# V terms of the context's expert sum at the delta net's priority on TensorE, and the lower parts of the query weights formed on VectorE

## The chip, the core and the metric

One core of a Trainium2 chip runs the whole program. The metric is the device time of one execution in microseconds. Five engines matter here: TensorE (PE, its weight loads PEld), VectorE (DVE), ScalarE (ACT), GpSimd (POOL) and the DMA queues, of which GpSimd issues the indirect ones and SyncE (SP) nearly all of the others. Each engine works through its own instructions in the order in which they were written into its queue; an instruction that waits holds up all that stand behind it on that engine.

## What is computed

Two layers over 512 latent tokens and 256 context tokens of width 1024. Layer 0 mixes with neighbourhood attention and a gated delta net, layer 1 with latent attention. Each layer ends with the same channel mixer, for latent tokens and (in layer 0) for context tokens, in which a token picks 16 experts per head among 16,384:

```
def peer_ffn(h, w_q, sub_keys, u_tab, v_tab):
    def one_block(xb):                                  # 128 tokens
        qy = (xb @ w_q).reshape(t, PEER_HEADS, 2, PEER_DKEY // 2)
        s = jnp.einsum('thpd,hpnd->thpn', qy, sub_keys)
        s_top, i_top = lax.top_k(s, kk)                 # 16 of 128, per half
        comb = s_top[:, :, 0, :, None] + s_top[:, :, 1, None, :]
        c_top, c_idx = lax.top_k(comb..., kk)           # 16 of 256
        expert = i1 * PEER_KEYS + i2
        gate = jax.nn.softmax(c_top, axis=-1)
        u, vv = u_tab[expert], v_tab[expert]
        act = jax.nn.gelu(jnp.einsum('td,thkd->thk', xb, u))
        return jnp.einsum('thk,thkd->td', gate * act, vv)
```

The delta net's scan, the other piece that the change touches, goes chunk by chunk: `u = w_v - w_k @ s; o = q_dec @ s + p_in @ u; s = b_end * s + k_end.T @ u`, after a triangular solve in each chunk.

## The kernel before

The program is traced in Python and a list scheduler then sorts the instructions of each engine by priority and estimated readiness. Priority falls with the place in the program; `high_priority(offset=k)` moves what is written under it ahead by k places. `LATER` is 4,194,304 (line 30), and `later()` (line 1231) is `high_priority(offset=-LATER)`: whatever stands under it comes last among what could run.

*Routes.* `peer_route` (from line 1030) finds each token's experts: `cp` for the 256 context tokens, `xp` and `yp` for the latent tokens of layers 0 and 1. Its queries are 16 feature blocks in four groups of four. For each block `query` loads a 1024x128 weight (`wq`), rounds it on ScalarE to the upper part (`wqh`, line 1068), subtracts to get the lower part (`wql`, line 1069), and runs 24 matmuls (`qy`). `choose` then scores the group against the sub-keys (`s`, copied to `sc`), and `top16` on VectorE reads each score row several times (`V`, `I`, `t_rep`). The four groups go one after the other: group 0's top-16 runs on VectorE while TensorE makes group 1's queries.

*Two ways to apply experts.* The context's two 128-token tiles, and one latent tile a layer, gather rows: `gather_slots` (from line 1227) yields, tile by tile, 128 steps of U and then 128 of V. Each step has GpSimd gather 128 rows of 1024 floats (512 KB) into one of six `row` buffers (line 1239); four steps later the row is used. A U row is one dot product on VectorE (`cp_jk`, line 1257). A V row is one multiply-add into an accumulator on VectorE (`cp_acc`, line 1282), but while the latent delta net runs (`self.spare`, set in `gdn`), every third one is a pair of matmuls on TensorE instead: ScalarE makes a diagonal matrix of the factors (`cp_dg`, line 1266) and TensorE adds diagonal times row into two banks (`cp_va`, line 1271). 18 V terms of the context's first tile go that way. The gather and the use of a row both stand under `later()`.

The other three latent tiles of each layer run all experts: `peer_dense` goes through 128 blocks, each with 512 KB of U and of V loaded by SyncE, scores, gates, and products on TensorE. ScalarE's rounding of each V block (`vh`, line 1410) marks one block in the trace; VectorE subtracts to get `vl` (line 1411).

*Pace of the gather.* A step is taken from the gather's queue by `pump(anchor, k)`: the gather then may not be issued ahead of the anchor instruction (an order only, no wait at run time), and k says how many steps to take. In the dense layer, each block takes three. `pump(x, 0)` takes none and only sets the anchor; that is what line 1069 does.

*Stages* (us in the trace): context route 335 to 500; latent mixer of layer 0 from there, with the delta net's projections 680 to 823, its scan in four parts (`x_c0` to `x_c3`, starting at 823, 882, 938 and 991) and the output projection (`x_o0` to `x_o3`, from 1074); latent route 1143 to 1503 with the first top-16 at 1179; dense layer 0 from 1519; mixer of layer 1 2560 to 2957; its route 2957 to 3322; dense layer 1 from there to the end.

Of the kernel before, what the change touches and what calls it, by code (L numbers as in the profile page):

```python
# [29 lines left out]
LATER = 1 << 22  # L30
# [10 lines left out]
class Trunk:  # L41
# [988 lines left out]
    def peer_route(self, layer, nm, xT, nd, beside=iter(())):  # L1030


        nc = self.nc
# [4 lines left out]
        with ExitStack() as st:  # L1038
# [10 lines left out]
            def half(t, g):  # L1049
                hs = slice(4 * g, 4 * g + 4)  # L1050
                return self.combine(c1, c2, V[t], Iu[t], ex[t], gate[t], hs, nm + f"_c{t}{g}")

            with ExitStack() as qst:
                w3 = qst.enter_context(self.tc.tile_pool(name=nm + "_prw", bufs=2))
                self.fills(1)
                q2 = qst.enter_context(self.tc.tile_pool(name=nm + "_prq", bufs=2))

                def query(fg):
                    sk = q2.tile([P, 4, P], F32, tag="sk", name=nm + f"_sk{fg}")
                    nc.sync.dma_start(sk, self.I["peer_sk"][layer, :, fg * 4:fg * 4 + 4, :])  # L1060
                    qy = q2.tile([P, 4, n], F32, tag="qy", name=nm + f"_qy{fg}")
                    for j in range(4):
                        f = fg * 4 + j
                        raw, wh, wl = [w3.tile([P, KD, P], dt, tag=tag, name=nm + f"_{tag}{f}")
                                       for tag, dt in (("wq", F32), ("wqh", F32R), ("wql", F32R))]
                        nc.sync.dma_start(raw, self.I[f"peer_w_q{layer}"][:, f * P:(f + 1) * P]
                                          .rearrange("(k p) n -> p k n", p=P))
                        nc.scalar.copy(wh, raw)
                        self.pump(nc.gpsimd.tensor_sub(wl, raw, wh), 0)
                        p = self.ps(nm + f"_qy{fg}{j}")  # L1070
                        for k in range(KD):
                            self.mm(p[:, :n], wh[:, k, :], xh[:, k, :], start=(k == 0), stop=False)
                            self.mm(p[:, :n], wh[:, k, :], xl[:, k, :], start=False, stop=False)
                            self.mm(p[:, :n], wl[:, k, :], xh[:, k, :], start=False, stop=(k == KD - 1))
                        nc.scalar.copy(qy[:, j, :], p[:, :n])
                        aside(1)
                    return qy, sk

                def choose(fg, qy, sk):
                    for t in order:  # L1080
                        p = self.ps(nm + f"_s{fg}_{t}")
                        for j in range(4):
                            self.mm(p[:, j * P:(j + 1) * P], qy[:, j, t * P:(t + 1) * P], sk[:, j, :])
                        sc = q2.tile([P, 4, P], F32, tag="sc", name=nm + f"_sc{fg}_{t}", bufs=4)
                        nc.scalar.copy(sc, p.rearrange("p (j k) -> p j k", k=P))
                        for j in range(4):
                            f = fg * 4 + j
                            self.top16(p2, sc[:, j, :], V[t][:, f, :], Iu[t][:, f, :], P, nm + f"_t{fg}{t}{j}")
                        aside(1)

                first = []

                def aside(k):
                    while k and first:
                        if next(first[0], 0) == 0:
                            first.pop(0)
                        else:
                            k -= 1

                for fg in range(4):  # L1100
                    choose(fg, *query(fg))
                    if fg == 2:
                        next(beside, None)
                    if fg == 1:
                        first += [half(t, 0) for t in order]
                while first:
                    aside(1)
                    self.fills(2)
# [118 lines left out]
    def gather_slots(self, xs, dst, routes, s, layer, nm):  # L1227
        nc, tc = self.nc, self.tc
# [32 lines left out]
        def v_use(act, gate, acc, j, t):  # L1261
            def use(v):
                if self.spare and j % 3 == 0 and 0 < j < P - 8:

                    dg = gp.tile([P, P], F32, tag="diag", name=nm + f"_dg{t}_{j}", bufs=2)
                    nc.scalar.mul(dg, self.ident, act[:, j:j + 1])
                    f, l = self.spare is True, j + 3 >= P - 8
                    if f:
                        self.spare = [self.acc(nm + f"_va{t}{h}") for h in range(2)]
                    for h, p in enumerate(self.spare):  # L1270
                        i = nc.tensor.matmul(p, dg, v[:, h * 512:(h + 1) * 512], start=f, stop=l)  # L1271
                    if l:
                        for h, p in enumerate(self.spare):
                            nc.vector.tensor_add(acc[:, h * 512:(h + 1) * 512], acc[:, h * 512:(h + 1) * 512], p)
                        self.spare = None
                    return i
                if j == 0:
                    nc.scalar.activation(act, act, AF.Gelu)
                    nc.vector.tensor_mul(act, act, gate)
                    i = nc.vector.tensor_scalar_mul(acc, v, act[:, 0:1])  # L1280
                else:
                    i = nc.vector.scalar_tensor_tensor(acc, v, act[:, j:j + 1], acc, op0=ALU.mult, op1=ALU.add)  # L1282
                if j == P - 1:
                    g2 = self.bcast(gp, layer, 2, 1, s, nm + f"_g2{t}", "row", bufs=6)
                    nc.vector.tensor_mul(acc, acc, g2)
                    x = gp.tile([P, D], F32, tag="row", name=nm + f"_gx{t}", bufs=6)
                    nc.sync.dma_start(x, xs[t])
                    nc.vector.tensor_add(acc, x, acc)
                    nc.sync.dma_start(dst[t], acc)
                return i  # L1290
            return use

        for t, (h2, idx, gate) in enumerate(routes):
            act = gp.tile([P, P], F32, tag="act", name=nm + f"_act{t}", bufs=2)
# [384 lines left out]
```

## Time and profile before

| | us |
|---|---|
| median of 3 runs (lowest, highest) | 4307.02 (4299.18, 4308.93) |
| the profiled execution, its own time | 4297.03 |
| its span on the core | 4295.0 |
| PE busy | 3966.5 (92%) |
| DVE busy | 3301.4 (77%) |
| POOL busy | 1725.9 (40%) |
| ACT busy | 1623.1 (38%) |

The mean granted clock of TensorE is 0.968 of full speed. Busy shares are means over stages with different limits, so a change in one stage is read from that stage's own rows. On the page, POOL's costliest work is the gathers (1.25 to 1.44 us of issuing each), and its longest waits are for row buffers to come free: 319.4 us ahead of the context's U gathers, 289.3 us ahead of its V gathers. DMA moved 1113.66 MB in all.

### The profile page before, as it was taken

The page shows a single profiled execution, that of the slowest core. Times are in us where ns is not written, and L with a number is a line of the kernel's source. Part 1 is how long each engine was busy: PE and PEld are TensorE (multiplying, and loading weights), DVE is VectorE, ACT ScalarE, POOL GpSimd, SP SyncE. Part 2 cuts the span into 40 slices and gives each one's busy share as a digit, 9 for nine tenths or more (in the row PEclk, how much of TensorE's full clock was granted, in tenths as well). Part 3 has the DMA queues.
Part 4 walks back from the last instruction along what each step waited for, and adds up shares of the span by engine and source line. Part 5 has one row for each costly group of instructions (what it writes and reads, how often), then busy time and mean ns, then how long its engine had stood idle before and what let it go on. Part 6 is the DMA issues. An engine that isn't in the chain of part 4 may idle for free.

```text
span 4295.0 us, 58812 instructions
## 1 busy us (share of the span) xinstructions
PE 3966.5 (92%) x20522; PEld 3209.9 (75%) x20522; DVE 3301.4 (77%) x7027; ACT 1623.1 (38%) x2947; POOL 1725.9 (40%) x1435
## 2 busy tenths in 40 slices
PE   7997888999899979999999978999999999999998
PEld 4676654687476768888888856775667899999987
DVE  1354988986699979999998886554998777777776
ACT  2353443355124623333333323552245333333333
POOL 0003366543330057777876663001100555555540
PEclk8999998999999989999999988999999999999999
DMA  9835498755634599999999997112246998998885
GB/s 307 293 113 148 161 323 305 284 189 172 204 117 147 220 392 394 396 395 390 394 382 356 331 347 254 47 45 91 78 160 239 362 309 304 309 311 307 308 301 192
DMA packets 484713, 1113.66 MB, mean 259 GB/s; under 512 B 38720, under 2 KB 256320, under 8 KB 475200
## 3 DMA queue, kind: packets, MB, share of 16 engines
q1 hardware_dynamic: 328752, 561.49, 38.0%
q0 software_dynamic: 147600, 537.40, 34.5%
q10 hardware_dynamic: 8064, 11.01, 0.7%
q8 instruction: 162, 2.65, 0.3%
q14 instruction: 135, 1.11, 0.1%
HBM read 1036.30 MB, written 73.92 MB: 258 GB/s over the span
## 4 chain that ended last, share of the span: by engine, by line
PE 56%; DVE 16%; DMA 14%; issue 7%; POOL 5%; ACT 2%; SPq 0%; POOLq 0%; DVEq 0%; ACTq 0%
PE yp_acc L77 11%; PE yp_sp L77 10%; PE xp_sp L77 4%; PE xp_acc L77 3%; DMA cp_u<-peer_u,cp_idx 3%; POOL xp_v L1239 2%; PE mq_s L77 2%; PE x_p L77 2%; DMA xp_u<-peer_u,xp_idx 2%; DMA xp_v<-peer_v,xp_idx 2%; DMA xp_ur<-peer_uT 1%; PE xp_pg L77 1%; PE yp_pg L77 1%; DMA xp_vr<-peer_v 1%; PE c_p L77 1%
## 5 line engine op out<-in xcount | busy, mean ns | idle before, releaser
L1239 POOL DMA_INDIRECT cp_u<-peer_u,cp_idx x256 | 318.9, 1246 | 319.4 <-DVE cp_jk L1257 236.2
L1239 POOL DMA_INDIRECT cp_v<-peer_v,cp_idx x256 | 329.1, 1286 | 289.3 <-PE cp_va L1271 100.3
L77 PE MATMUL xp_sp<-xp_xT,xp_uh 128*128 128x384 f32 x1600 | 409.9, 337 | 16.0 <-ACT xp_ge L1476 14.0
L77 PE MATMUL yp_sp<-yp_xT,yp_uh 128*128 128x384 f32 x1600 | 412.2, 339 | 3.5 <-ACT yp_uh L1372 1.8
L1316 POOL COPY tick<-yp_vh 128x1 f32<-128x1 f32 x104 | 117.5, 1130 | 518.2 <-ACT yp_vh L1410 518.2
L77 PE MATMUL xp_acc<-xp_vh,xp_ah 128*128 128x512 f32 x768 | 305.0, 397 | 20.7 <-ACT xp_ah L1421 20.6
L77 PE MATMUL xp_acc<-xp_vh,xp_al 128*128 128x512 f32 x768 | 307.9, 401 | 15.5 <-DVE xp_al L1422 14.8
L1282 DVE SCALAR_TENSOR_TENSOR cp_acc<-cp_v,cp_act,cp_acc 128x1024 f32<-128x1024 f32 x236 | 302.3, 1281 | 19.4 <-DMA cp_v<-peer_v,cp_idx 17.1
L77 PEld LDWEIGHTS xp_sp<-xp_xT,xp_uh 128*128 128x128 f32 x1600 | 293.0, 189 | 24.6 <-ACT xp_ge L1476 14.6
L77 PE MATMUL xp_acc<-xp_vl,xp_ah 128*128 128x512 f32 x768 | 303.6, 395 | 0.4 <-DVE xp_vl L1411 0.3
L77 PE MATMUL yp_acc<-yp_vh,yp_al 128*128 128x512 f32 x768 | 299.7, 390 | 2.1 <-DVE yp_al L1422 2.0
L77 PEld LDWEIGHTS yp_sp<-yp_xT,yp_uh 128*128 128x128 f32 x1600 | 292.3, 187 | 12.1 <-ACT yp_ge L1476 2.3
L77 PE MATMUL yp_acc<-yp_vh,yp_ah 128*128 128x512 f32 x768 | 299.3, 390 | 0.7 <-ACT yp_ah L1421 0.7
L77 PE MATMUL yp_acc<-yp_vl,yp_ah 128*128 128x512 f32 x768 | 299.1, 389 | 0.0
L1411 DVE TENSOR_TENSOR yp_vl<-yp_vr,yp_vh 128x1024 fp32r<-128x1024 f32 x128 | 156.8, 1225 | 152.8 <-ACT yp_vh L1410 152.7
L77 PE MATMUL yp_sp<-yp_xT,yp_ul 128*128 128x384 f32 x800 | 270.9, 339 | 0.9 <-DVE yp_ul L1373 0.9
L77 PE MATMUL xp_sp<-xp_xT,xp_ul 128*128 128x384 f32 x800 | 270.0, 338 | 0.0
L1421 ACT CAST xp_ah<-xp_a 128x384 fp32r<-128x384 f32 x128 | 65.7, 513 | 431.8 <-DVE xp_a L1417 415.3
L1372 ACT CAST yp_uh<-yp_ur 128x1024 fp32r<-128x1024 f32 x100 | 105.1, 1051 | 294.8 <-PE yp_sp L77 270.6
L1239 POOL DMA_INDIRECT xp_v<-peer_v,xp_idx x128 | 184.8, 1444 | 54.7 <-DVE xp_acc L1282 33.2
L1239 POOL DMA_INDIRECT xp_u<-peer_u,xp_idx x128 | 178.5, 1394 | 64.2 <-DVE xp_jk L1257 30.8
L77 PEld LDWEIGHTS xp_acc<-xp_vh,xp_al 128*128 128x128 f32 x768 | 145.6, 190 | 65.0 <-DVE xp_al L1422 35.0
(1483 smaller groups left out, 10543.9 us busy)
## 6 DMA issues: line engine op xcount, KB each, us to landing
xp_ur<-peer_uT SPq DMA_DIRECT2D x128, 512.0 KB, 6.9
xp_vr<-peer_v SPq DMA_DIRECT2D x128, 512.0 KB, 7.0
yp_ur<-peer_uT SPq DMA_DIRECT2D x128, 512.0 KB, 5.4
yp_vr<-peer_v SPq DMA_DIRECT2D x128, 512.0 KB, 4.4
aw<-ada_w SPq DMA_DIRECT2D x48, 1024.0 KB, 6.9
gdram<-xp_go SPq DMA_DIRECT2D x12, 2048.0 KB, 7.5
xp_gb<-gdram SPq DMA_DIRECT2D x32, 768.0 KB, 11.4
gdram<-yp_go SPq DMA_DIRECT2D x12, 2048.0 KB, 7.1
```

The source lines that it names most:

```text
L77: self.nc.tensor.matmul(out, lhsT, rhs, start=start, stop=stop)
L1239: d = nc.gpsimd.indirect_dma_start(out=r, out_offset=None, in_=tab, in_offset=bass.IndirectOffsetOnAxis(ap=idx[:, j:j + 1], axis=0))
L1282: i = nc.vector.scalar_tensor_tensor(acc, v, act[:, j:j + 1], acc, op0=ALU.mult, op1=ALU.add)
L1316: self.pump(self.nc.gpsimd.tensor_copy(t, src[:, 0:1]), k)
L1372: nc.scalar.copy(uh, uv)
L1411: nc.vector.tensor_sub(vl, vr, vh)
L1421: nc.scalar.copy(ah, a)
```

## The change

Two edits. The diagonal and the two matmuls of a TensorE V term are written under `high_priority(offset=LATER)`, inside the `later()` that already surrounds every use of a row: the two cancel, and these instructions get the priority of the place at which they are written, in the delta net's scan. The gather of the row, and all VectorE uses, stay under `later()`. And `wql` is subtracted on VectorE instead of GpSimd, in all three routes, 16 times each; it remains the anchor.

```diff
@@ -1066,7 +1066,7 @@
                         nc.scalar.copy(wh, raw)
-                        self.pump(nc.gpsimd.tensor_sub(wl, raw, wh), 0)
+                        self.pump(nc.vector.tensor_sub(wl, raw, wh), 0)
@@ -1263,12 +1263,14 @@
                     dg = gp.tile([P, P], F32, tag="diag", name=nm + f"_dg{t}_{j}", bufs=2)
-                    nc.scalar.mul(dg, self.ident, act[:, j:j + 1])
+                    with tc.high_priority(offset=LATER):
+                        nc.scalar.mul(dg, self.ident, act[:, j:j + 1])
                     f, l = self.spare is True, j + 3 >= P - 8
                     if f:
                         self.spare = [self.acc(nm + f"_va{t}{h}") for h in range(2)]
-                    for h, p in enumerate(self.spare):
-                        i = nc.tensor.matmul(p, dg, v[:, h * 512:(h + 1) * 512], start=f, stop=l)
+                    with tc.high_priority(offset=LATER):
+                        for h, p in enumerate(self.spare):
+                            i = nc.tensor.matmul(p, dg, v[:, h * 512:(h + 1) * 512], start=f, stop=l)
```

TensorE before, at the end of the output projection (`x_o3p` products of the last tile, `h2T` transposes of the normed tiles), where the last V term stands:

```order
L77 MATMUL x_o3p_9188<-x_wo_8995,x_yT 128x512 x4
L77 MATMUL x_o3p_9188<-x_wo_8999,x_yT 128x512 x4
L80 MATMUL x_o2h2T_9218<-ident,x_o2h 128x128 x4
L80 MATMUL x_o2h2T_9226<-ident,x_o2h 128x128 x4
L1271 MATMUL cp_va_6511<-cp_v_117_7135,cp_dg_117_7193 128x512
L80 MATMUL x_o3h2T_9234<-ident,x_o3h_9215 128x128 x4
L80 MATMUL x_o3h2T_9241<-ident,x_o3h_9215 128x128 x4
```

TensorE after, in the delta net's third part (`x_c2`, the steps of its triangular solve), where the same term and the one before it stand:

```order
L77 MATMUL x_c2pt_7866<-x_c2X,x_c2Bm 128x128 x4
L1273 MATMUL cp_va_6511<-cp_v_114_7053,cp_dg_114_7140 128x512
L77 MATMUL x_c2py_7872<-x_c2dec,x_c2Y 128x128 x4
L1273 MATMUL cp_va_6510<-cp_v_117_7135,cp_dg_117_7193 128x512
L77 MATMUL x_c2py_7878<-x_c2dec,x_c2Y 128x128 x4
L80 MATMUL x_c2px_7884<-ident,x_c2X 128x128 x4
L77 MATMUL x_c2pt_7908<-x_c2X,x_c2Bm 128x128 x2
L1273 MATMUL cp_va_6511<-cp_v_117_7135,cp_dg_117_7193 128x512
L77 MATMUL x_c2pt_7908<-x_c2X,x_c2Bm 128x128 x2
```

The last V term moved from behind the output projection into the third of the scan's four parts, between matmuls of its chain.

GpSimd before, at the latent route's first `wql` (the context's last V gathers, its second tile's first U gathers):

```order
L1239 DMA cp_v_122_7199<-peer_v,cp_idx_3765 128x1024
L1239 DMA cp_v_123_7202<-peer_v,cp_idx_3765 128x1024
L1069 TENSOR_TENSOR xp_wql_9313<-xp_wq_9311,xp_wqh_9312 128x1024
L1239 DMA cp_v_124_7219<-peer_v,cp_idx_3765 128x1024
L1239 DMA cp_v_125_7222<-peer_v,cp_idx_3765 128x1024
L1069 TENSOR_TENSOR xp_wql_9345<-xp_wq_9343,xp_wqh_9344 128x1024
L1239 DMA cp_v_126_7225<-peer_v,cp_idx_3765 128x1024
L1239 DMA cp_v_127_7228<-peer_v,cp_idx_3765 128x1024
L1239 DMA cp_u_0_7258<-peer_u,cp_idx_3833 128x1024
```

GpSimd after, at the latent route's end (`xp_gk` is the copy of its gates, the last thing before the dense layer):

```order
L1239 DMA cp_u_104_8594<-peer_u,cp_idx_3833 128x1024
L1239 DMA cp_u_105_8598<-peer_u,cp_idx_3833 128x1024
L1118 COPY xp_gk_10744<-xp_gate_9293 128x128
L1239 DMA cp_u_106_8602<-peer_u,cp_idx_3833 128x1024
L1239 DMA cp_u_107_8606<-peer_u,cp_idx_3833 128x1024
```

Of the second tile's 128 U gathers, 106 stand ahead of that copy now, and 22 before the change.

VectorE before, at the first tile of the output projection (`x_o0t` scales the product, `x_o0x` adds the input, `x_o_*` and `x_o0h` norm it):

```order
L1274 TENSOR_TENSOR cp_acc_5507<-cp_acc_5507,cp_va_6510 128x512
L738 TENSOR_TENSOR x_o0t_9021<-x_o0p_9012,x_g_9001 128x512
L739 TENSOR_TENSOR x_o0x<-x_o0x,x_o0t_9021 128x512
L738 TENSOR_TENSOR x_o0t_9033<-x_o0p_9024,x_g_9001 128x512
L739 TENSOR_TENSOR x_o0x<-x_o0x,x_o0t_9033 128x512
L121 TENSOR_SCALAR x_o_v<-x_o_ssq 128x1
L124 RECIPROCAL x_o_y<-x_o_y 128x1
L126 TENSOR_TENSOR x_o_t<-x_o_y 128x1
```

VectorE after, at the second tile of it (`xp_xT` is the transposed normed tile that the route reads):

```order
L739 TENSOR_TENSOR x_o1x<-x_o1x,x_o1t_9065 128x512
L748 TENSOR_TENSOR x_o0h<-x_o0h,x_SH_9007 128x1024
L1257 SCALAR_TENSOR_TENSOR cp_jk_52_7966,cp_act_7257<-cp_u_52_7922,c_o1h_2503 128x1024
L1257 SCALAR_TENSOR_TENSOR cp_jk_53_7970,cp_act_7257<-cp_u_53_7926,c_o1h_2503 128x1024
L738 TENSOR_TENSOR x_o1t_9077<-x_o1p_9068,x_g_9001 128x512
L1257 SCALAR_TENSOR_TENSOR cp_jk_54_7974,cp_act_7257<-cp_u_54_7930,c_o1h_2503 128x1024
L739 TENSOR_TENSOR x_o1x<-x_o1x,x_o1t_9077 128x512
L759 TENSOR_TENSOR xp_xT_8988<-x_o0h2T_9098,xp_xT_8987 128x4x128
```

U rows of the second context tile stand between the projection's own steps, where none stood. In whole stretches: from `x_c1` to `x_o0`, 55 V rows where 42 were and 44 U rows where none were; from `x_o0` to the route's first top-16, 48 U rows where 10 were, none of the 13 V rows that were there, and 6 `xp_wql`; in the route's top-16, 8 U rows where 6 were, and 10 `xp_wql` (4, 4 and 2 ahead of its second, third and fourth group).

VectorE after, in the route of layer 1, between the top-16 of group 0 (`yp_V_24583`) and that of group 1 (`yp_V_24584`):

```order
L1146 MATCH_REPLACE yp_t_rep<-yp_V_24583,yp_sc_2_24840 128x128
L1069 TENSOR_TENSOR yp_wql_24935<-yp_wq_24933,yp_wqh_24934 128x1024
L1147 MAX yp_V_24583<-yp_t_rep 128x8
L1069 TENSOR_TENSOR yp_wql_24967<-yp_wq_24965,yp_wqh_24966 128x1024
L1148 MAX_INDEX yp_I_24587<-yp_V_24583,yp_t_rep 128x8
L1069 TENSOR_TENSOR yp_wql_25126<-yp_wq_25124,yp_wqh_25125 128x1024
L1069 TENSOR_TENSOR yp_wql_25169<-yp_wq_25167,yp_wqh_25168 128x1024
L1143 MAX yp_V_24584<-yp_sc_3_25002 128x8 x2
```

The first two are the lower parts of group 1's third and fourth block: TensorE can finish group 1's queries only when VectorE has come to the end of group 0's top-16.

## Rows read from the trace of the kernel before

**Rows 1.** Page, span in 40 slices: VectorE's busy tenths, the DMA engines' busy tenths.

```profile
DVE  1354988986699979999998886554998777777776
...
DMA  9835498755634599999999997112246998998885
```

**Rows 2.** Windows: stretch, length, PE, PEld, DVE, ACT, POOL busy, PEclk, DMA share, GB/s.

```profile
740.00:830.00 90.00, 85.75 (x345) 56.52 (x343) 85.14 (x115) 32.59 (x57) 65.02 (x67) 0.99 0.92 333
823.00:882.00 59.00, 48.10 (x341) 44.59 (x341) 52.30 (x73) 26.34 (x60) 27.07 (x23) 0.86 0.66 219
882.00:938.00 56.00, 52.72 (x415) 47.14 (x414) 43.19 (x69) 29.01 (x70) 19.67 (x17) 1.00 0.54 174
938.00:991.00 53.00, 52.94 (x418) 47.54 (x417) 39.92 (x67) 29.85 (x71) 18.51 (x15) 1.00 0.42 133
991.00:1074.00 83.00, 77.61 (x503) 60.55 (x502) 59.99 (x112) 40.66 (x116) 33.74 (x28) 0.98 0.61 191
1074.00:1143.00 69.00, 53.42 (x148) 25.72 (x147) 42.28 (x65) 12.34 (x24) 11.87 (x7) 0.89 0.46 145
1143.00:1179.00 36.00, 31.81 (x146) 25.82 (x145) 22.91 (x31) 8.87 (x13) 24.90 (x18) 0.92 0.90 306
1179.00:1268.00 89.00, 78.51 (x364) 64.57 (x363) 88.89 (x508) 23.64 (x35) 37.02 (x20) 0.96 0.40 126
1268.00:1503.00 235.00, 226.99 (x1199) 166.69 (x1199) 234.13 (x795) 118.60 (x238) 7.27 (x5) 0.99 0.48 176
1519.00:1622.00 103.00, 85.12 (x404) 74.21 (x403) 82.68 (x125) 30.33 (x42) 65.02 (x53) 0.92 1.03 387
1622.00:2406.00 784.00, 760.03 (x3762) 675.80 (x3761) 723.19 (x908) 259.78 (x362) 566.13 (x444) 1.00 1.01 383
3403.00:4151.00 748.00, 748.00 (x3777) 685.01 (x3776) 579.88 (x694) 269.14 (x360) 399.26 (x315) 1.00 0.90 308
```

**Rows 3.** Waits, 882 to 1144 and 882 to 1074 us: total, times, longest.

```profile
POOL cp_v L1239 <- PE cp_va L1271: 100.3, 10, 54.7
...
PE cp_va L1271 <- DMA cp_v<-peer_v,cp_idx: 2.6, 1, 2.6
```

**Rows 4.** One line's instructions, 823 to 1503 us: ns least/median/most, first and last start.

```profile
L1257 DVE SCALAR_TENSOR_TENSOR cp_jk<-cp_u,c_o1h x22: 1214/1224/3267, 1158.8 to 1502.2; 128x1024 bf16<-128x1024 f32 x22
...
L1282 DVE SCALAR_TENSOR_TENSOR cp_acc<-cp_v,cp_act,cp_acc x74: 1272/1280/1287, 822.1 to 1148.3; 128x1024 f32<-128x1024 f32 x74
```

**Rows 5.** The same view, rounding of V blocks, one per dense block, in three stretches.

```profile
L1410 ACT CAST xp_vh<-xp_vr x11: 1040/1046/1051, 1519.0 to 1621.5; 128x1024 fp32r<-128x1024 f32 x11
...
L1410 ACT CAST xp_vh<-xp_vr x91: 1032/1049/1055, 1621.5 to 2405.6; 128x1024 fp32r<-128x1024 f32 x91
...
L1410 ACT CAST yp_vh<-yp_vr x90: 1046/1047/1048, 3402.8 to 4143.2; 128x1024 fp32r<-128x1024 f32 x90
```

**Rows 6.** The same view: the subtraction on GpSimd, and its like on VectorE.

```profile
L1069 POOL TENSOR_TENSOR xp_wql<-xp_wq,xp_wqh x16: 2380/2412/2991, 1131.1 to 1249.5; 128x1024 fp32r<-128x1024 f32 x16
...
L1411 DVE TENSOR_TENSOR xp_vl<-xp_vr,xp_vh x128: 1212/1221/1227, 1524.3 to 2544.1; 128x1024 fp32r<-128x1024 f32 x128
```

**Rows 7.** Timeline, 1125 to 1140 us: start, duration, engine, instruction [idle before].

```profile
1131.13 2.99 POOL L1069 TENSOR_TENSOR xp_wql<-xp_wq,xp_wqh 128x1024 fp32r<-128x1024 f32 x1 [4.35 <-DMA x<-x_o3x]
1131.84 2.30 DVE L130 TENSOR_TENSOR x_o_r<-x_o_y,x_o_t 128x1 f32<-128x1 f32 x1
...
1137.65 3.35 DVE L748 TENSOR_TENSOR x_o3h<-x_o3h,x_SH 128x1024 f32<-128x1024 f32 x1
```

**Rows 8.** Timeline, 3008 to 3022 us, and the chain there (start, length, engine).

```profile
3010.12 0.28 DVE L1148 FIND_INDEX8 yp_I<-yp_V,yp_t_rep 128x8 uint32<-128x128 f32 x1
...
3017.44 0.49 DVE L1143 MAX8 yp_V<-yp_sc 128x8 f32<-128x128 f32 x2 [7.04 <-ACT yp_sc L1085]
...
2992.47 22.40 PE yp_qy L77 x96
```

## The prediction

> **What bounds the kernel now.** I read the page's slices first: VectorE is full through the context's gather and again in the latent route, the DMA engines are full in the dense layer of layer 0 and have room while the delta net runs [rows 1]. Then the table by stage, to see which engine each stage waits for. In the projections, 740 to 830, VectorE is busy 85.14 of 90 us (94.6%) with TensorE; at the scan's first part 52.30 of 59 (89%); from 882 to 1074 it falls to 43.19 + 39.92 + 59.99 = 143.10 of 192 us, with DMA at 0.42 to 0.61 [rows 2]. So there is room in the scan, and the waits say who leaves it empty: GpSimd waited 100.3 us ahead of V gathers for the TensorE terms, 54.7 us of it in one piece [rows 3]. In the output projection and up to the first top-16 (1074 to 1179) VectorE does 42.28 + 22.91 = 65.19 of 105 us. In the route's top-16 it is the bound, 88.89 of 89 and 234.13 of 235 us [rows 2].
>
> In dense layer 0 the DMA engines are the bound: a block takes (1621.5 - 1519.0)/10 = 10.3 us over the first ten, then (2405.6 - 1621.5)/90 = 8.71 us, at 383 to 387 GB/s and a share of 1.01 to 1.03. In layer 1 a block takes (4143.2 - 3402.8)/89 = 8.32 us with TensorE busy for 748.00 of 748 us and DMA at 0.90 [rows 2, 5]. What the gathers cost layer 0 against that pace is 10 x 2.0 + 90 x 0.39 = 55 us. That is the most that rows moved out of it can give back.
>
> **V terms at the delta net's priority.** The 36 matmuls and 18 diagonals are the same; what moves is their place, and with it when row buffers come free. GpSimd then runs on: by the orders VectorE gets 13 more V rows and 44 more U rows between x_c1 and x_o0. At 1.280 and 1.224 us [rows 4] that is 16.6 + 53.9 = 70.5 us, and 143.1 + 70.5 = 213.6 us of work for a stretch of 192. VectorE takes its queue in order, so what stands ahead of x_o0 is done ahead of it: the stretch grows by 22 us even if VectorE never idles. At the 94.6% of the projections it takes 225.8 us, **+34**; at the 89% of the scan's first part 240, **+48** [rows 2]. The scan's steps hand over between TensorE and VectorE, so some idling stays; but a row of 1.2 us fits its gaps, as in the projections. I take **+37**, near the first, ends +22 and +48. If TensorE's chain were all that counts, the 70 us would be hidden and the term nought; I don't use that, since 213.6 us of work don't fit into 192.
>
> From x_o0 to the route's first top-16: 38 more U rows (46.5 us), 13 V rows fewer (-16.6), six subtractions come to VectorE at 1.221 us [rows 6] (7.3), and three long stretches there go (next part, -6.3): 65.2 + 46.5 - 16.6 + 7.3 - 6.3 = 96.1 of 105 us, 92%. It fits, but rows now stand between the norms of four tiles that the route waits for. **+3**, ends 0 (all in gaps) and +12 (ten rows in the way).
>
> In the dense layer 28 U rows of the second tile are left at its start instead of 128 - 22 = 106 [rows 4]. Before, the surplus over the three rows a block was worked off slowly over nearly all blocks. After, by VectorE's order it is gone after some 17 blocks, and the rest runs at three rows, as in layer 1. If the first ten blocks stay as slow and seven more lose 0.39, 23 us of the 55 remain: gain 32. If the first ten shrink with the surplus (28/106 of 20 us), 8 remain: gain 47. If only the later loss shrinks, in step with rows, 35 x 78/106 = 26. I take **-38**, ends -26 and -50.
>
> **Lower parts on VectorE.** 48 subtractions of 2.41 us leave GpSimd, 48 of about 1.22 us (the like for `vl`) come to VectorE [rows 6]: 58.6 us in all, priced by where they fall. Something comes back: where a GpSimd subtraction overlapped a VectorE instruction with two inputs, the latter was stretched; x_o_r on 128x1 took 2.30 us beside the subtraction at 1131.13, x_o3h 3.35, and one cp_jk 3.27 against a median of 1.22 [rows 4, 7]. I counted about a dozen such instructions, some 2 us each: 6 us in the context's route, 11 from x_o3 on in the latent route (6.3 ahead of its first top-16, 4.8 behind), 4 in layer 1's.
>
> The Trainium skill ("SBUF — State Buffer", Who interferes with whom) says that a VectorE instruction with two SBUF inputs contends with a GpSimd instruction that reads SBUF; the stretched rows agree. If all 48 had blocked VectorE for 2 us, 96 us would come back against 58.6, a gain; the trace shows a dozen, 21 us, so I keep the rows' count. The skill's "Perfetto Trace Analysis" (Optimizing Scalar/DVE Operations) warns that offloading between these two might not help, for the same port; that would leave the sum's sign open, as I have it.
>
> Latent route of layer 0: ten subtractions in the top-16 (12.2) and two more rows (2.5), less 4.8 of stretches: 9.9 us on an engine that is full. **+9**, ends +5 (rows that stood behind this stretch have gone, and the six subtractions ahead of it may let it start sooner) and +12.
>
> Route of layer 1: in the order, the lower parts of group 1's last two blocks stand at the end of group 0's top-16, which ends at 3010.4 [rows 8]. Then one subtraction (1.2), the two blocks' matmuls at 22.40/4 = 5.6 us each, scores and copy (2.5): 3010.4 + 1.2 + 11.2 + 2.5 = 3025.3 against 3017.44 before, +8 on a wait of 7.04 us that grows [rows 8]. Behind it VectorE is full, and gets six subtractions (7.3) less 4 of stretches: +3. Some of it returns where the other subtractions go into that wait. **+9**, ends -2 and +12.
>
> Context route: VectorE is busy for 0.4 of the slice from 322 to 429 us, in which most of its queries fall, and for 0.9 of the next [rows 1]. 16 x 1.22 = 19.6 us come to it, ten of the 16 within the top-16 by the order, against 6 us of stretches and subtractions of half the length for TensorE to wait for. **0**, ends -6 and +8; what hides them is the idle time of the first slice, and without it the price is 10 x 1.22 - 6 = 6 or more.
>
> **Sum.** 37 + 3 - 38 + 9 + 9 + 0 = **+20 us**. Against the profiled execution's 4297 that is 4317; the four runs that I have (4297.0, 4299.2, 4307.0, 4308.9) have a mean of 4303, and the profiled one is at their low end, so I add to 4303: **4323 us**. Ends by the terms, all one way: -26 + 48 and so on would give -31 to +66; together they seldom fall so, and I take +3 to +42 (4306 to 4345) for this case.
>
> **Rivals.** *The scan takes the rows in its gaps, and the dense layer gives the more* (chance 0.27). VectorE waits 192 - 143 = 49 us in the scan; packed to 100% the stretch grows by 22, the projection by 0, the routes by 5 + 0 + 0, and the dense layer gives 45: -18, some **4285**. For it: the rows are short, the gaps many, and the projections run at 94.6%. Against: no stretch with the scan's steps is over 89% in the trace. It decides where the scan's growth stays below about 24 us and the dense gain passes 40.
>
> *TensorE waits for rows in the middle of the scan* (0.13). A V term now stands between matmuls of the solve, and its row must have landed. The one such wait in the trace is 2.6 us [rows 3]; if each of 18 terms costs that, 47 us go onto the chain, and VectorE's added work fits only partly beside it: 22 + 47 = 69 in place of 37, the sum +52, **4355**. Against: GpSimd has six buffers and less to wait for, so rows come early. It decides once most terms wait.
>
> *Nothing moves* (0.10): the rows' earlier place in the order is not used, since they land as late as before and what the scan gains the dense layer loses: scan and dense near nought, routes +9 at most, **4303 to 4310**.
>
> Forecast as summed: 0.50.
>
> **How the numbers follow.** About 0.2% (8.6 us) is what a measurement of this kernel can tell from no change: 4298 and 4316 are the borders. The forecast's range has some 0.35 of 0.50 above 4316, 0.14 between, 0.01 below; the first rival 0.23 below and 0.04 between; the second 0.13 above; the last between, 0.09. Faster 0.24, same 0.27, slower 0.49. The range must reach into both neighbours, since faster and slower hold three quarters together: 4280 to 4355; the forecast's own is 4306 to 4345.
>
> **What would show it.** In the profile after: the waits of GpSimd for cp_va fall from 100.3 to below 20 us; the stretch from x_c1 to x_o0 takes 225 to 240 us with VectorE at 90 to 95% (first rival: 214 to 217; second: TensorE's waits for cp_v over 30 us); cp_jk starts inside the scan; the dense layer's blocks come to 8.3 us after the first 20 (8.7 means that the surplus is still there); the wait ahead of the second group's top-16 in layer 1 is about 12 us instead of 7; and no VectorE instruction of 2 us beside a subtraction. I am wrong if the scan does not grow, or if the first ten dense blocks, whose slowness I don't take apart, carry the gain.

## The result, and the profile after

| | before | after |
|---|---|---|
| median (lowest, highest), us | 4307.02 (4299.18, 4308.93) | 4339.89 (4338.57, 4340.44) |
| ratio to before, 95% interval | | 1.0083 (1.0066 to 1.0099) |
| span of the profiled execution, us | 4295.0 | 4338.1 |
| PE, DVE, ACT, POOL busy, us | 3966.5, 3301.4, 1623.1, 1725.9 | 3973.6, 3338.6, 1641.1, 1585.0 |

The change costs 33 us, 0.83%. The profiled execution of before was at the low end of its runs, so the two traces differ by more, 43 us. They can be laid side by side by the first start of an instruction that opens each stage. This table is worked out from such starts: the length of each stage before, and how much longer it is in other kernels (the two edits alone are the first two experiments below). A column adds up to the difference of two single executions (+43, +42 and +22 us), where the medians differ by 33, 26 and 6; how much of an entry belongs to the one execution no run shows.

In the table `x_c1` and `x_c3` open with the first `x_c1dec` and `x_c3dec` on VectorE. `x_o0` opens here with the first `x_o0x`, which in the trace of before waits 9.7 us for a transfer; the prediction counts from `x_o0t`, 10.4 us earlier. By the prediction's mark x_c1 to x_o0 takes 192.1 us before and 253.2 after (+61.1, where the table has 51.3 + 7.2), and x_o0 to the first top-16 104.6 and 113.2 (+8.6).

| stage (first start to first start) | before, us | after | V terms only | subtractions only |
|---|---|---|---|---|
| start to first cp_jk (context route) | 503.4 | +8.2 | +2.4 | +14.5 |
| to x_c1 | 378.6 | -4.1 | -0.6 | +0.1 |
| x_c1 to x_c3 | 108.8 | **+51.3** | +47.7 | -0.3 |
| x_c3 to x_o0 | 93.7 | +7.2 | +11.2 | -0.8 |
| x_o0 to first top-16 of xp | 94.2 | +11.2 | +9.0 | -1.5 |
| to first dense block, layer 0 | 340.4 | +10.8 | +0.4 | +8.6 |
| first ten blocks | 102.5 | -19.6 | -5.2 | -17.4 |
| next ninety | 784.1 | -32.1 | -30.5 | +9.8 |
| to first top-16 of yp | 585.7 | +3.0 | +5.9 | +2.7 |
| to first dense block, layer 1 | 330.2 | +13.3 | 0.0 | +13.1 |
| first ten blocks | 81.3 | -7.7 | +0.6 | -9.6 |
| to the last block | 866.3 | +1.5 | +1.5 | +2.8 |

The largest entry is the scan's middle. The windows of x_c1 to x_c3, before and then after (columns as in [rows 2]):

```profile
882.00:990.80 108.80, 105.46 (x828) 94.48 (x827) 82.91 (x135) 58.86 (x141) 38.17 (x32) 1.00 0.48 154
```

```profile
886.10:1046.20 160.10, 136.38 (x893) 111.71 (x892) 120.80 (x166) 64.06 (x151) 81.42 (x70) 0.95 0.72 239
```

Before, TensorE is busy for 105.46 of 108.80 us: this part of the scan was bound by TensorE. After, it is busy for 31 us more, yet stands idle for 24. VectorE got its 38 us more, and stands idle for 39. Work alone, without any wait, would need 136.38 us on TensorE and 120.80 on VectorE, so at least 28 us of the growth are set by TensorE's busy time; VectorE's alone would have asked for 12. The groups of the V terms there, before and after (line, engine, operation, count | busy, mean ns | idle ahead of it and until what):

```profile
L1271 PE MATMUL cp_va<-cp_v,cp_dg 128*128 128x512 f32 x30 | 15.4, 594 | 0.0
```

```profile
L1273 PE MATMUL cp_va<-cp_v,cp_dg 128*128 128x512 f32 x72 | 39.7, 636 | 15.4 <-DMA cp_v<-peer_v,cp_idx 14.5 <-ACT x_c1X L652 0.8
L1273 PEld LDWEIGHTS cp_va<-cp_v,cp_dg 128*128 128x128 f32 x72 | 11.4, 199 | 18.9 <-DMA cp_v<-peer_v,cp_idx 16.2 <-issue 1.7 <-ACT x_c1X L652 0.9
```

All 72 matmul records of the V terms now lie in this stretch, where 30 lay: 24 us more of TensorE's time. And TensorE waits 14.5 us for rows to land, where it waited for none.

The windows above also show the granted clock, with a mean of 1.00 before and 0.95 after. In three pieces TensorE was granted the lower of its two levels, 1.2 instead of 2.4 GHz: the windows 914 to 918, 976 to 980 and 1000 to 1010 us have a mean of 0.57, 0.58 and 0.50. Ahead of each it had been idle for much of the time: busy for 2.41 of 6, 2.08 of 4 and 1.57 of 4 us. A mean of 0.95 over 160.1 us is some 16 us at the lower level, which by estimate costs up to 8 us; the mean V record of 636 ns instead of 594 is part of it. So a part of the 31 us is the clock's, which fell after the waits; no run here separates the two.

The chain that ended last shows how one such wait for a row comes about (start, length, what):

```profile
906.52 1.45 POOL cp_v L1239
...
908.63 5.43 DMA cp_v<-peer_v,cp_idx
...
914.10 1.73 PE cp_va L1273 x2
915.82 1.71 PE x_c1pt L77 x8
```

GpSimd issues the gather when a buffer comes free, the row lands 5.4 us later, and the scan's own product `x_c1pt` stands behind the V term that waits for it; for the last 2.1 us of that TensorE is idle. The gather waits in turn for VectorE's use of an older row, among the scan's steps; the waits of the same stretch (total, times, longest):

```profile
POOL cp_v L1239 <- DVE cp_acc L1284: 23.3, 14, 5.0
...
POOL cp_v L1239 <- PE cp_va L1273: 12.7, 5, 6.5
```

GpSimd's wait for cp_va has shrunk from 100.3 us [rows 3] to these 12.7, as the change intends. The dense blocks answer to [rows 5]:

```profile
L1412 ACT CAST xp_vh<-xp_vr x11: 1041/1051/1054, 1603.7 to 1686.6; 128x1024 fp32r<-128x1024 f32 x11
```

```profile
L1412 ACT CAST xp_vh<-xp_vr x91: 1041/1052/1057, 1686.6 to 2438.6; 128x1024 fp32r<-128x1024 f32 x91
```

The first ten take 8.3 us each (10.3 before), the next ninety 8.36 (8.71). In the route of layer 1 the chain after reads, for three of the four groups in the same way:

```profile
3045.70 1.14 DVE yp_wql L1069
3046.89 12.06 PE yp_qy L77 x44
3058.95 1.11 PE yp_s L77 x10
3082.90 1.14 DVE yp_wql L1069
3084.08 12.04 PE yp_qy L77 x44
```

A subtraction at the end of one group's top-16, then 12 us of queries, then scores, while VectorE has no top-16 to work on.

### The profile page after: what moved, and what is told of

The parts are those of the page before. It is cut to its first block, busy times and chain, and to the rows that moved or that the text cites. A ratio compares the mean times of both kernels' runs of the same rounds, so it can differ in the third digit from the quotient of the medians.

```text
span 4338.1 us, 58780 instructions
## 1 busy us (share of the span) xinstructions
PE 3973.6 (92%) x20522; PEld 3220.7 (74%) x20522; DVE 3338.6 (77%) x7075; ACT 1641.1 (38%) x2953; POOL 1585.0 (37%) x1387
## 4 chain that ended last, share of the span: by engine, by line
PE 59%; DVE 14%; issue 12%; DMA 10%; ACT 3%; POOL 2%; SPq 0%; DVEq 0%; ACTq 0%; POOLq 0%
PE yp_acc L77 11%; PE yp_sp L77 11%; PE xp_sp L77 7%; PE xp_acc L77 7%; DMA cp_u<-peer_u,cp_idx 2%; PE mq_s L77 2%; DMA xp_vr<-peer_v 2%; DVE cp_acc L1284 2%; PE yp_qy L77 1%; DMA cp_v<-peer_v,cp_idx 1%; DVE cp_jk L1257 1%; PE yp_pg L77 1%; PE x_p L77 1%; PE c_p L77 1%; PE ada_ps L77 1%
## 5 line engine op out<-in xcount | busy, mean ns | idle before, releaser
L1239 POOL DMA_INDIRECT cp_u<-peer_u,cp_idx x256 | 309.1, 1208 | 386.3 <-DVE cp_jk L1257 280.6
L1239 POOL DMA_INDIRECT cp_v<-peer_v,cp_idx x256 | 318.5, 1244 | 187.1 <-DVE cp_acc L1284 87.7
L77 PE MATMUL xp_acc<-xp_vh,xp_ah 128*128 128x512 f32 x768 | 302.9, 394 | 13.4 <-ACT xp_ah L1423 11.2
L1413 DVE TENSOR_TENSOR xp_vl<-xp_vr,xp_vh 128x1024 fp32r<-128x1024 f32 x128 | 156.7, 1224 | 107.7 <-ACT xp_vh L1412 103.9
L1318 POOL COPY tick<-xp_vh 128x1 f32<-128x1 f32 x128 | 135.5, 1059 | 228.4 <-ACT xp_vh L1412 227.8
L1412 ACT CAST xp_vh<-xp_vr 128x1024 fp32r<-128x1024 f32 x128 | 134.5, 1051 | 175.2 <-PE xp_acc L77 96.0
L1374 ACT CAST xp_uh<-xp_ur 128x1024 fp32r<-128x1024 f32 x100 | 105.3, 1053 | 244.7 <-PE xp_sp L77 205.9
```

What stands on the lines that cost most here:

```text
L77: self.nc.tensor.matmul(out, lhsT, rhs, start=start, stop=stop)
L1239: d = nc.gpsimd.indirect_dma_start(out=r, out_offset=None, in_=tab, in_offset=bass.IndirectOffsetOnAxis(ap=idx[:, j:j + 1], axis=0))
L1318: self.pump(self.nc.gpsimd.tensor_copy(t, src[:, 0:1]), k)
L1374: nc.scalar.copy(uh, uv)
L1412: nc.scalar.copy(vh, vr)
L1413: nc.vector.tensor_sub(vl, vr, vh)
```

## The experiments

Each run was compared with runs of the kernel before on the same chip (medians 4305.78, 4302.58 and 4303.27 us in the three sessions). In the expectations, theory W is mine at the outset (VectorE's work for the rows lengthens the scan), L says that TensorE's waits for rows do, L2 and M, formed on the way, that TensorE's chain does: its matmuls and its waits for rows together.

### The two edits apart

V terms only:

```diff
-self.pump(nc.vector.tensor_sub(wl, raw, wh), 0)
+self.pump(nc.gpsimd.tensor_sub(wl, raw, wh), 0)
```

> Only the V terms of TensorE get the delta net's priority; the lower parts stay on GpSimd. Theory W (the scan grows by the VectorE work of the rows that now stand in it, the routes by the subtractions): x_c1 to x_o0 grows as in the changed kernel (+59 us, within 6), the dense layer of layer 0 gives about -50, the latent route and layer 1's route come back to before (their +11 and +6 go), so 4307 + 10 to 22 us. Rival P (the subtractions cost most of the 33 us): within 5 us of the kernel before. Both: the dense blocks run at 8.3 us after the first 25.

Measured: 4331.48 us, ratio 1.0058 (1.0038 to 1.0077), +25.7. The scan grows by 58.9 us up to x_o0, and both routes are as before; the dense layer gives 35.7, not 50, so the total lies above the expected 10 to 22. Rival P, which put most of the price on the subtractions, falls.

Subtractions only (the diff's first edit on the kernel before):

> Only the subtractions go to VectorE; the V terms keep the gather's late priority. Theory W: scan and dense layer as before (x_c1 to x_o0 within 4 us, dense blocks at 8.7), context route +4, latent route +9 to 11, layer 1's route +13 with 6 to 8 of it given back in the first ten dense blocks: 4307 + 15 to 24 us. Rival P: +30 or more. A third possibility (the subtractions on GpSimd stretched VectorE as much as they now cost it): +0 to 5.

Measured: 4312.22 us, ratio 1.0016 (1.0001 to 1.0030), +6.4: less than expected. The context route pays 14.5, the latent route 8.6 and layer 1's 13.1; but the first ten dense blocks give back 17.4 and 9.6. Part of the reason can be counted: while its queries wait, TensorE works ahead on the dense layer's scores. Ahead of the first V block 430 matmul records of xp_sp had started in the kernel before and 475 here, 10.3 us of TensorE's time, and 29 gelu records instead of 26. In layer 1 it is 477 records for 439, 9.8 us, which covers the 9.6; in layer 0 it leaves 7 of the 17.4 open. So the first ten blocks repay the price of the two latent routes, and the context route's is left, which has no such work behind it. The 9.8 us by which the next ninety blocks of this trace are longer are not explained; beside the V terms the subtractions leave them as they are (-32.1 with, -30.5 without). 25.7 + 6.4 = 32.1: within the intervals the two edits add up to the change.

### What lengthens the scan

U rows of the second tile held back until the output projection has ended:

```diff
 def pump(self, anchor, k):
+    if self.held: self.short += k; return
...
     row(U, idx, j, ...)
+    if s == 1 and t == 1 and j == 3: self.held = True
...
 turn(len(xs) - 1, h)        # end of out_proj
+self.held = False; self.pump(self.last_sub, self.short)
```

> The changed kernel, but of the second context tile's U rows only four may be gathered before the output projection of the latent mixer has ended; the rest follow from there on. So the scan holds the TensorE V terms at their new places and 13 more V rows on VectorE, but not the 44 U rows. Theory W: x_c1 to x_o0 grows by 15 to 28 us instead of 59, x_o0 to the first top-16 by less than 5; the dense layer starts with some 90 rows left and gives at most -10, so the whole is +35 to +60 against before. Rival L (the V terms' waits for rows on TensorE, in the middle of the scan's chain, make the growth): x_c1 to x_o0 still grows by 45 us or more.

Measured: 4337.45 us, ratio 1.0078 (1.0054 to 1.0102). x_c1 to x_o0 grows by 34.7 us, between the two theories. The parts tell more: x_c1 to x_c3 still grows by 44.9, while x_c3 to x_o0, which now holds no row at all, becomes 10.2 us shorter than before. The 44 U rows all stand in x_c3; they cost 7.2 + 10.2 = 17 us, 0.4 us a row for rows of 1.22 us. So they are not what lengthens the middle.

TensorE V terms on a resident tile:

```diff
-i = nc.tensor.matmul(p, dg, v[:, h * 512:(h + 1) * 512], start=f, stop=l)
+i = nc.tensor.matmul(p, dg, routes[t][0][:, h * 512:(h + 1) * 512], start=f, stop=l)
```

> The changed kernel, but the TensorE V terms multiply a tile that is always resident in place of the gathered row (so these 18 terms of the sum are wrong); the rows are still gathered, and nobody reads them. TensorE then waits for no row. Theory W: the scan keeps nearly all of its growth, x_c1 to x_o0 shrinks by at most 10 us against the changed kernel. Rival L: it shrinks by 16 us (the waits of TensorE for cp_v that the trace shows) to 40 (with what follows from them).

Measured: 4338.44 us, ratio 1.0078 (1.0050 to 1.0107). x_c1 to x_o0 is 13.8 us shorter than in the changed kernel, x_c1 to x_c3 alone 21.2: without the waits for rows 21 us of the 51 go, and 30 remain. By the numbers on record neither theory is confirmed. And the gain stays in that stretch: x_c3 to x_o0 gives 7.4 us of it back, and the whole, at +32.7 us (22 to 46), is not measurably shorter than the changed kernel.

No TensorE terms at all (from the kernel before):

```diff
-self.spare = not s
+self.spare = False
```

> The kernel before with all V terms of the context on VectorE: no diagonals, no matmuls on TensorE. GpSimd then waits for no matmul either, and VectorE's order holds 45 V rows in x_c1 and x_c2 where 23 were, and 24 V and 18 U in x_c3. Theory L2: TensorE, busy for 105 of 109 us from x_c1 to x_c3, loses some 12 us of matmuls and waits for no row, so in spite of 28 us more on VectorE the stretch grows by less than 20 us (the changed kernel: 51). Rival W (VectorE's work sets it): 83 + 28 = 111 us at the 75% of the changed kernel, so +35 or more.

Measured: 4299.35 us, ratio 0.9997 (0.9988 to 1.0006). This decides against W in the scan's middle: x_c1 to x_c3 holds 45 V rows on VectorE instead of 23 and takes 109.0 us instead of 108.8. Its window:

```profile
880.10:989.10 109.00, 97.15 (x800) 90.49 (x799) 107.87 (x156) 57.11 (x134) 55.97 (x46) 1.00 0.68 219
```

VectorE is busy for 107.87 of 109.00 us, 99%, beside the scan's own steps, at no cost there. All of its idle time could be filled. Further on the rows are not free: x_c3 to x_o0, with 24 V and 19 U rows where 18 V rows stood, is 16.3 us longer, and the output projection 5.5; the dense layer gives 21.5 back.

V terms narrowed to 64 of 512 columns, waits and places kept:

```diff
-i = nc.tensor.matmul(p, dg, v[:, h * 512:(h + 1) * 512], start=f, stop=l)
+i = nc.tensor.matmul(p[:, :64], dg, v[:, h * 512:h * 512 + 64], start=f, stop=l)
```

> The changed kernel, but each TensorE V term covers 64 of every 512 columns (so most of these 18 terms of the sum are left out); the matmuls still wait for their gathered rows and stand at the same places, and 40 V rows stand on VectorE from x_c1 to x_c3 (51 in the changed kernel, 45 without TensorE terms). Theory M: the 51 us by which x_c1 to x_c3 grows are TensorE's: 42 more matmul records there of 0.594 us (25 us) on an engine that was busy for 105 of 109, and 16 us of waits for rows, the rest what follows from them. Without the matmuls' time the stretch grows by 10 to 28 us. Rival L (waits for rows alone): by 40 or more. Rival W (VectorE's rows): by 35 or more.

Measured: 4321.99 us, ratio 1.0036 (1.0021 to 1.0051). x_c1 to x_c3 grows by 23.4 us: theory M's range, and neither L's nor W's. The window and TensorE's wait:

```profile
889.60:1021.80 132.20, 110.02 (x870) 103.73 (x869) 103.63 (x152) 62.47 (x150) 66.75 (x59) 0.95 0.70 234
```

```profile
PE cp_va L1273 <- DMA cp_v<-peer_v,cp_idx: 16.1, 12, 4.4
```

With TensorE's time nearly back at before's (110 us for 105) and the waits still 16 us, 28 of the 51 us are gone, and the whole is at +18.7 instead of +33. Together with the resident tile: some 28 us go with the matmuls' time, some 21 with the waits for rows. The order differs here (40 V rows on VectorE for 51, and x_c3 to x_o0 5 us longer than in the changed kernel), and the clock's part goes with either, so these are sizes, not exact shares: up to x_o0 they are 23 and 14 us.

### Which terms to lift

Only the last six, and only the last three, of the 18 terms at the delta net's priority, subtractions on GpSimd:

```diff
-with tc.high_priority(offset=LATER):
+with tc.high_priority(offset=LATER if j >= 102 else 0):     # or 111
```

> Subtractions on GpSimd. Of the 18 TensorE V terms only the last six (rows 102 to 117) get the delta net's priority; the twelve before them keep the gather's. By VectorE's order the scan's parts x_c1 and x_c2 keep the rows of before (13 and 10 V rows), and the rows run on in x_c3 (28 V, 13 U) and the output projection (46 U). Theory L2 (the scan's first parts are bound by TensorE's chain, and each row that must land or be used inside them lengthens it; the later stages have room): x_c1 to x_c3 within 5 us of before, x_c3 to x_o0 +8 to +18, x_o0 to the first top-16 +8 to +12, dense layer -30 to -38, the whole -3 to -15. Rival W (each extra row costs its VectorE time wherever it stands ahead of the dense layer): x_c3 to x_o0 +28 or more, the whole +5 to +25.

> The same with only the last three terms (rows 111, 114, 117) at the delta net's priority: x_c3 holds 28 V rows and no U row, the output projection 41 U rows. Theory L2: x_c1 to x_c3 within 5 us, x_c3 to x_o0 +3 to +12, x_o0 to the first top-16 +5 to +12, dense layer -20 to -32, the whole -3 to -15. Rival W: x_c3 to x_o0 +13 or more, the whole +0 to +20.

Measured: last six 4316.27 us, ratio 1.0037 (1.0023 to 1.0051); last three 4301.30, ratio 1.0001 (0.9991 to 1.0012). Both leave x_c1 to x_c3 as it was (0.0), as L2 expects. But with six, x_c3 to x_o0 grows by 27.4 us, which is close to W's number, and the dense layer gives only 18.1. With three it grows by 8.7, the projection by 7.3, and the dense layer gives 15.7: nothing is won. What makes the six so dear the trace shows at the end of x_c3. There the scan's result is normed on VectorE in short steps that follow one another (`x_on_*`, then `x_oa`), and TensorE can transpose only what is normed. The waits of the last six, and then of the changed kernel from x_c3 to x_o0:

```profile
PE x_oT L80 <- DVE x_oa L700: 16.2, 2, 14.1
```

```profile
PE x_oT L80 <- DVE x_oa L700: 13.5, 2, 8.0
```

Before, this wait is 0.7 us; without TensorE terms it is 21.2. In VectorE's order a U row of 1.22 us stands between nearly every two of those steps: from `x_on_v` to the end of `x_oa` the second norm takes 3.9 us before and, with six rows in between, 10.1 with the last six terms. So theory W holds in this place: not by the rows' sum, but where they stand between short dependent steps.

### The subtraction's place in the queue

Subtractions on VectorE, with their rounding written 1000 places earlier in priority:

```diff
-nc.scalar.copy(wh, raw)
-self.pump(nc.vector.tensor_sub(wl, raw, wh), 0)
+with self.tc.high_priority(offset=1000):
+    nc.scalar.copy(wh, raw)
+    sub = nc.vector.tensor_sub(wl, raw, wh)
+self.pump(sub, 0)
```

> Only the subtractions go to VectorE, but with the rounding on ScalarE ahead of them they are written with a priority 1000 places earlier, so that in VectorE's order they no longer stand behind the whole top-16 of the group before. Theory Q (TensorE's queries wait because the subtraction is queued behind the top-16): the context route's growth of 13 us falls to 0 to 4, that of layer 1's route (first top-16 to first dense block) from 13 to under 5; the whole within 5 us of before. Rival R (the 16 x 1.22 us of VectorE work themselves are the price): the context route stays at +8 or more, layer 1's at +9 or more, the whole at +6 or more.

Measured: 4299.38 us, ratio 0.9991 (0.9982 to 1.0001). The context route's growth falls from 14.5 to 1.2 us, that of layer 1's route from 13.1 to 4.3: theory Q. The same subtractions on the same engine cost 9 to 13 us less in a route when they don't stand behind the top-16. In the context's route the 14th block shows it: behind the top-16 its subtraction starts at 449.5 us, 12.5 after its rounding has started, and with the earlier priority at 424.4, 2.6 after it; the last query matmul starts at 461.1 and 442.5. TensorE's waits for the subtractions themselves, at the end of the top-16 and ahead of it, are only part of that:

```profile
PEld cp_qy L77 <- DVE cp_wql L1069: 8.4, 4, 5.7
```

```profile
PEld cp_qy L77 <- DVE cp_wql L1070: 4.6, 4, 2.7
```

Behind the top-16 TensorE waits another 11.1 us for roundings, and ScalarE 35.1 us for the weights that it rounds (28.4 with the earlier priority). The rounding's own earlier priority was not tried without the subtraction's.

### Together

No TensorE terms and the earlier subtractions; and the same with six terms (rows 66 to 96, every sixth) left on TensorE at the late priority:

```diff
-self.spare = not s                                    # none
+self.spare = False
-if self.spare and j % 3 == 0 and 0 < j < P - 8:       # six
+if self.spare and j % 6 == 0 and 0 < j < 100:
```

> No TensorE V terms, and the subtractions on VectorE with the earlier priority: the two variants that did not lose, together. Theory M: x_c1 to x_c3 within 4 us of before; projection and route +15 to 25 for some 55 more U rows, dense layer -20 to -30; layer 1's route +4 with as much given back in its first dense blocks; the whole -10 to +4 against before. If the two collide (both fill VectorE in the latent route): +5 to +15.

> Subtractions on VectorE with the earlier priority; only six V terms of the context (rows 66 to 96, every sixth) on TensorE, at the gather's late priority. Theory M: x_c1 to x_c3 within 5 us of before, or up to 4 shorter, since TensorE and VectorE are both below what they carried in the kernels before and without terms; the whole -12 to +4. If a late term holds up the gather as before: x_c1 to x_c3 +5 or more, with GpSimd waiting for cp_va over 40 us.

Measured: none 4299.68 us, ratio 0.9988 (0.9979 to 0.9998); six 4300.39, ratio 0.9993 (0.9983 to 1.0002). The first is the fastest ratio of the study, 0.12% below before, which is hardly more than the measurement can tell; it beats the changed kernel, at 1.0083, by 0.9%. Its parts are near what M expects: x_c1 to x_c3 +0.3 us, projection and latent route +14.3, dense layer -29.7, layer 1's route +4.2. With six terms the whole is inside M's range, but x_c1 to x_c3 grows by 10.8 us though GpSimd waits for cp_va only 2.6 us: neither expectation for that stretch holds. Its window:

```profile
877.80:997.40 119.60, 107.95 (x824) 97.45 (x824) 111.66 (x160) 58.42 (x138) 61.71 (x53) 0.97 0.71 233
```

VectorE's 111.66 us of work are more than the 108.8 that the stretch took before. With 46 V rows there it is full, as it was with 45 and no TensorE terms; 3 of the 10.8 us follow from that, the others were not taken apart.

## Why the prediction was right, and where it was not

The time (4339.89 for a range of 4280 to 4355) and the direction came out as forecast, and the forecast's own range, 4306 to 4345, holds it. The sum was too small, +20 where the medians moved by 33 and the two traces by 43. Its largest term was right in direction for a wrong reason, and outside its own ends. That the time still fell into the range is in part luck: the scan grew by over 20 us more than the term says, and the dense layer gave 14 us more.

- **Scan, +37 (22 to 48): measured +61.1 by the prediction's mark, +58.5 in the table.** The step that failed is the sentence that the 36 matmuls "are the same; what moves is their place", costed at nothing. They moved into two stretches in which TensorE was busy for 52.72 of 56 and 52.94 of 53 us, rows that stood in [rows 2] and that I read only for VectorE. Priced from the trace, 42 more records of 0.594 us are 25 us; the narrowed matmuls took 28 off the stretch.
- **VectorE's share, which set the term between its ends.** The floor of 22 us was nearer 15: VectorE's busy time over the stretch came to 206.67 us, not 213.6 (three of the 13 "V rows" are other additions into the same accumulator, and neighbouring instructions overlap). What lay above it was not VectorE's idling between hand-overs: without TensorE terms VectorE reached 99% in x_c1 to x_c3, above the 94.6% and 89% that I took from other stages, and in the changed kernel it was at 75%, 29.6 of its 38.3 us of waits being for TensorE. Of the rows' own work 22 more V rows cost x_c1 to x_c3 nothing as long as VectorE had room for them, and the 44 U rows, all in x_c3, 17 us, with 13.5 us of TensorE's waits for the norm between them.
- **The rival in which TensorE waits for rows** named the second cause and its place, and priced it at 2.6 us for each of 18 terms, 47 us. The trace shows 14.5 us of it on TensorE, in 8 waits, less than the 30 us that were its sign; taking it away gave 21 in x_c1 to x_c3, 14 up to x_o0, and nothing measurable in the whole. I gave it 0.13 as a world of its own; it was a part of the likeliest one. By size the scan's 61 us are nearer its 69 than my 37.
- **Projection, +3 (0 to 12): measured +8.6 by the prediction's mark, +11.2 in the table**, towards the upper end: TensorE waits 22.2 us for the normed tile `x_o3h` and 11.1 for `x_o0h` (before 15.6 and none), so the rows did get in the way of the norms, as the bound said. VectorE also waited 12.2 us for U rows to land between x_c3 and the first top-16 (9 waits), which I had not counted.
- **Dense layer, -38 (-26 to -50): measured -51.7** with both edits, -35.7 with the V terms alone. The term itself was right. The other 16 us come with the subtractions' longer route, which I did not see: 476 score records stand ahead of the first V block, 441 with the V terms alone, some 10 us of TensorE's time. A delayed stage let the next one start further on.
- **Latent route, +9 (5 to 12): measured +10.8.** Right.
- **Layer 1's route, +9 (-2 to 12): measured +13.3**, less 7.7 in its first dense blocks. The mechanism was as worked out for one group (VectorE's step from its top-16 to the next took 13.2 us instead of 7.04); three groups show it.
- **Context route, 0 (-6 to +8): measured +8.2 in the changed kernel and +14.5 alone.** The cover that I named, idle time in VectorE's slice, does not help: the subtraction waits for its place in the order, behind top-16 instructions. The order showed it there as plainly as in layer 1, where I did use it.
- **The stretched VectorE instructions came back.** Of those that take over 0.3 us longer than the median of their kind, the trace before has 10 with 18.1 us in all, each beside a subtraction on GpSimd (I had counted about a dozen with 21; the context's route has 2.9 us of it, not 6). The traces with the subtractions on VectorE have none. In the changed kernel the longest cp_jk from x_c3 to the first top-16 takes 1.247 us where 3.267 was the most before [rows 4]:

```profile
L1257 DVE SCALAR_TENSOR_TENSOR cp_jk<-cp_u,c_o1h x92: 1174/1224/1247, 1046.8 to 1251.4; 128x1024 bf16<-128x1024 f32 x92
```

The Trainium skill ("SBUF — State Buffer", Who interferes with whom) says that a VectorE instruction with two SBUF inputs contends with a GpSimd instruction that reads SBUF. This agrees: with the subtractions gone from GpSimd, the 10 long ones are gone too. The Trainium skill's "Perfetto Trace Analysis" (Optimizing Scalar/DVE Operations) warns that offloading between the two might not help, since they share a port. The runs agree with the caution (+6.4 us), but not through the port, which gave VectorE 18.1 us back: in another place of the queue the same move is within the noise (-3.2 us).

Of what should have shown the forecast right: the waits for cp_va did fall below 20 us, dense blocks did come to 8.4, and no long VectorE instruction remained; but the stretch took 253 us, not 225 to 240, and VectorE did not run at 90 to 95% in it (75% in x_c1 to x_c3, 87% in x_c3, 82% in all), and that is the mark of the wrong reason.

## What to carry to other kernels

Before costing a move at nothing, look at the engine that executes the moved instruction in the stretch that it moves into, not only at the engine that it frees. Filler work whose data come late (a gathered row) belongs on an engine with idle time there and late in its order: from x_c1 to x_c3 the V terms were free on VectorE and cost 50 us in the middle of TensorE's chain, and over the whole kernel they made no measurable difference on VectorE (ratio 0.9997). Keep it out of runs of short dependent steps: there six rows of 1.22 us lengthened a norm of 3.9 us by 6.2. When a small producer changes engines, read where it stands in the new queue: 48 instructions of 1.2 us cost 6 us behind the top-16, and nothing that could be measured ahead of it.

## What the runs showed beyond that

- 36 fp32 matmuls of 128x512 leave 72 records of 0.594 us at the full granted clock. Neighbouring records overlap (30 of them keep TensorE busy for 15.4 us), so one V term, two matmuls, is some 2.1 us of TensorE. On VectorE the same term takes 1.28 us.
- VectorE was 99% busy with rows of 1.28 us between the scan's own steps, and the stretch stayed the same within 0.3 us.
- A route that is 9 to 13 us longer gave back 8 to 17 us in the ten dense blocks behind it; some 10 us of that are scores with which TensorE filled its wait.
- Ten VectorE instructions that met a GpSimd subtraction of 2.4 us took 0.7 to 2.1 us longer than their like, and none did where the subtraction ran on VectorE.
